# One hybrid encoder layer on one core: an output tile's norm in six parts over the next pair, an opening in another order, a map's weights made earlier

## The chip, the cores and the metric

The kernel runs on one core of a Trainium2 chip. The core's engines take their instructions in order, each from a queue of its own, and meet at semaphores: TensorE (PE; PEld is its weight load), VectorE (DVE), ScalarE (ACT), GpSimd (POOL) and SyncE (SP), whose queue issues most DMAs. The metric is the device time of one execution in microseconds, the median of several runs.

## What is computed

One encoder layer over 4096 tokens of width 1024, with 16 meta tokens put in front and dropped at the end. In the reference, cut:

```python
h = jnp.concatenate([meta, x], axis=1)
u = rmsnorm(h, norm_g[i])
proj = jnp.einsum('bld,de->ble', u, w_in[i])
f_in, f_gate, q, k, v, a_gate = jnp.split(proj, SPLIT_POINTS, axis=-1)
f_out = fourier_branch(f_in, w_fmix[i], b_fmix[i]) * jax.nn.silu(f_gate)
a_out = attention_branch(q, k, v, q_norm_g[i], k_norm_g[i], cos, sin, n_tok) * jax.nn.silu(a_gate)
mixed = jnp.concatenate([f_out, a_out], axis=-1)
h = h + jnp.einsum('ble,ed->bld', mixed, w_out[i])
h = rmsnorm(h, final_g)
return h[:, N_META:]
```

`fourier_branch` is the real part of a 2-D DFT over the positions and the 64 channels of each of 8 groups, followed by a 64 x 64 map of each group. `attention_branch` has 8 query heads and 2 key heads of width 64, with a norm of q and k and a rotary embedding, softmax over all 4112 keys.

## The kernel before

**The first part (up to some 729 us)** projects the tokens in 33 tiles of 128. Operands are split into a high and a low half of 16 bits (`wh`, `wl` for weights, `xh`, `xl` for tokens), and each product takes three matmuls. The first three tiles (meta, 0, 31), the opening, are written out by hand in the order in which their pieces come: `wsplit` makes a quarter of the split weights of a group of columns (`GB` is the last group; ScalarE makes `wh` at line 271, VectorE `wl` at line 272), `tile_q`, `tile_gate` and the like are the matmuls of a tile's columns, `tile_norm` is the norm of q and k on VectorE (lines 355 to 380), `tile_stack` writes keys and values into their layout, `stat` and `stat_end` are the row statistics of the next tiles (squares with a sum on ScalarE at line 201, a root on VectorE from line 211, transposes on TensorE at line 219, a copy at 221), `xload` and `xsplit` load and split a token tile (line 289). After that a loop goes over the remaining tiles with four slots each, in which a table, `plan`, puts the folding of the Fourier weights and the loads for the second part (`at(slot, step)` adds a step).

**The second part (729 us to the end)** has two things in it. First the DFT over positions of one channel group after another (`f_step`), with the group's map (lines 84 to 86: three matmuls with `wvh`, `wvl` and the split transform `thl`); the map's weights are made by `fix_load` (DMAs) and `fix_prep` (VectorE, ScalarE) at the start of this part. Then 32 pairs: a block of 512 queries (b) and two heads (p), each with 66 positions j (33 key tiles, two heads). At a position TensorE makes s (lines 1043 and 1044, two buffers), ScalarE its exp (line 1047), GpSimd or VectorE the remainder `rr` of that exp (line 1049: VectorE at the positions two behind those of the list `AT`, GpSimd at the others), and five positions later TensorE uses them with the values (lines 1064 to 1071). At the sixteen positions of `AT`, TensorE makes two groups of scores for the row maxima of the next pair (line 975, two buffers `m`, both groups behind each other) and VectorE reduces each (line 976).

**The output tile.** Beside this, each pair from the fifth on finishes one output tile of 128 tokens of the block before: transposes at position 12 (`mh` on ScalarE, `ml` on VectorE at 13), the product with the output weights in two halves at positions 15 to 38 and 39 to 62, each ending with `hh` (line 1129). Then the final norm: `square` (ScalarE, line 1141, with the sum of a row in `ss`) at position 62, `root` (ten operations of VectorE on one column, lines 1144 to 1166: a first guess by integer operations and three Newton steps) at position 3 of the next pair, `scale` (VectorE, line 1149, and the store of the tile) at position 14. After the last pair a tail does the last block's tiles.

What sets the order in the second part is the loop itself: instructions reach an engine's queue in the order in which the loop's body writes them, position by position.

Of the kernel before, what the change touches and what calls it, by code (L numbers as in the profile page):

```python
# [22 lines left out]
F32 = mybir.dt.float32  # L23
# [105 lines left out]
def phase_a(tc, a, pool, mm3, id16, id32, sc):  # L129
# [15 lines left out]
    with ExitStack() as st:  # L145
# [359 lines left out]

        PER, SLOTS = 12, 4
# [37 lines left out]
        at(b + 8, ld["acs_load"], 0)  # L544
        done = 27
# [80 lines left out]
        tile_norm(31)  # L626
# [3 lines left out]
        tile_stack(0)  # L630
        wsplit(*GB, 2)
        stat_load(14)
        wsplit(*GB, 3)
        tile_gate(31, 768, fg_d)
        tile_tr(NT)
        stat_store(order[:3])
        tile_stack(31)
# [10 lines left out]
        tile_gate(0, 1280, ag_d)  # L648
        xsplit(15)
        xload(16)  # L650
# [28 lines left out]
def phase_b(tc, a, pool, mm3, id32, id16, sc):  # L679
# [10 lines left out]
    with ExitStack() as st:  # L690
# [53 lines left out]
        wst, wv = (w2.tile([P, 2, 4, P], F32, tag="xr", name=n) for n in ("wst", "wv"))  # L744
        wvh, wvl = (w1.tile([P, 2, 4, P], F16, tag=t, name=n) for t, n in (("mh", "wvh"), ("ml", "wvl")))
# [5 lines left out]
        sgn = bp.tile([P, 2], F32, name="sgn")  # L751
        stk8 = stk8.rearrange("p (g c)->p g c", c=P)

        def fix_load():
            dma(wst, a["wst"])
            dma(sgn, a["sgn"])
            dma(bias, a["bias"])

        def fix_prep():
            V.memset(stk8[0:64], 0.0)  # L760
            V.scalar_tensor_tensor(out=wv[:, 0], in0=wst[:, 0], scalar=sgn[:, 0:1], in1=wst[:, 1],
                                   op0=ALU.mult, op1=ALU.add)
            V.scalar_tensor_tensor(out=wv[:, 1], in0=wst[:, 1], scalar=sgn[:, 0:1], in1=wst[:, 0],
                                   op0=ALU.mult, op1=ALU.add)
            S.activation(wvh, wv, AF.Copy, scale=WS)
            V.scalar_tensor_tensor(out=wvl, in0=wv, scalar=WS, in1=wvh, op0=ALU.mult, op1=ALU.subtract)
# [334 lines left out]
        def out_tr(b, s):  # L1101
# [6 lines left out]
            mh = w1.tile([P, 8, P], F16, tag="mh", name="mh")  # L1108
            ml = w1.tile([P, 8, P], F16, tag="ml", name="ml")
# [24 lines left out]
        def out_end(b, s, d):  # L1134
# [8 lines left out]
            def root():  # L1143
                V.tensor_scalar(out=ss, in0=ss, scalar1=1.0 / D, scalar2=EPS, op0=ALU.mult, op1=ALU.add)
                rsqrt1(sm, rf, ss)
# [7 lines left out]
            return square, root, scale  # L1153

        def rsqrt1(p, y, x):

            t = p.tile([P, 1], F32, tag="r1t", name="r1t")
            h = p.tile([P, 1], F32, tag="r1h", name="r1h")
# [5 lines left out]
            for _ in range(3):  # L1164
                V.tensor_scalar(out=t, in0=y, scalar1=y, scalar2=h, op0=ALU.mult, op1=ALU.mult)
# [65 lines left out]
        for i, (b, p) in enumerate(pairs):  # L1231
# [16 lines left out]
            for j, (qk, pvm) in enumerate(stream(i)):  # L1248
# [26 lines left out]
                if j == TR + 2 and prev:  # L1275
                    prev[2]()
# [199 lines left out]
```

## Time and profile before

| | |
|---|---|
| runs | 3283.27, 3285.66, 3286.85 us; median 3285.66 |
| the profiled execution | 3286.26 us, its span 3284.5 |
| mean granted clock of TensorE | 0.997 |
| TensorE busy (weight loads beside it) | 3216.3 us, 98% (1901.5, 58%) |
| VectorE busy | 2391.6 us, 73% |
| GpSimd busy | 2290.1 us, 70% |
| ScalarE busy | 1701.2 us, 52% |

The rows below are from that one execution. A row of a timeline has the start in us from the span's start, the duration, the engine, the line, the operation, what it writes and reads, and how many such instructions in a row; brackets hold the idle time of the engine just before and what ended it.

### The profile page before, as it was taken

To read this page: it belongs to the slowest core of one execution; us is meant where nothing else is said; L and a number is where in the kernel's file an instruction comes from. 1 tells how busy PE (TensorE), PEld (TensorE's weight loads), DVE (VectorE), ACT (ScalarE), POOL (GpSimd) and SP (SyncE) were. 2 spreads that over 40 slices of the span, in tenths; PEclk is the share of its full clock that TensorE was granted. 3 is DMA by queue.
4 is the path that set the end of the run, shared out by engine and by line. 5 is a ranking of instruction groups with operands and counts; after the bars stand their busy time and mean duration, and the time that the engine had idled before them with its cause. 6 is when DMAs were issued, how large, how long until landed. Compare 5 with 4: busy or idle time off the path is not lost.

```text
span 3284.5 us, 78548 instructions
## 1 busy us (share of the span) xinstructions
PE 3216.3 (98%) x33109; PEld 1901.5 (58%) x33109; DVE 2391.6 (73%) x3225; ACT 1701.2 (52%) x2967; POOL 2290.1 (70%) x2171
## 2 busy tenths in 40 slices
PE   7999999998999999999999999999999999999998
PEld 4555555656666555555555555555555555555564
DVE  6666566437667878777777778877777777887764
ACT  5443443333555555555555555555555555555563
POOL 3655555435777878777777777877787777877762
PEclk9999999999999999999999999999999999999999
DMA  6453343348422220010001000200100010010001
GB/s 223 147 165 128 135 165 109 108 143 260 130 81 84 66 62 27 30 46 21 21 21 47 21 21 24 55 28 21 46 21 21 21 46 21 24 32 25 21 21 58
DMA packets 133848, 225.66 MB, mean 69 GB/s; under 512 B 21654, under 2 KB 76774, under 8 KB 128886
## 3 DMA queue, kind: packets, MB, share of 16 engines
q1 hardware_dynamic: 119670, 195.47, 19.0%
q10 hardware_dynamic: 13824, 25.17, 2.0%
q8 instruction: 259, 4.24, 0.5%
q14 instruction: 95, 0.78, 0.1%
HBM read 159.46 MB, written 61.14 MB: 67 GB/s over the span
## 4 chain that ended last, share of the span: by engine, by line
PE 84%; DVE 10%; ACT 2%; DMA 2%; issue 1%; POOL 1%; SPq 0%; ACTq 0%; DVEq 0%; POOLq 0%
PE s L1043 12%; PE s L1044 12%; PE o L1064 11%; PE po L1124 9%; PE m L975 7%; PE o L1071 7%; PE ps L301 5%; PE ps L302 5%; PE ps L304 4%; DVE mx L976 4%; PE pd L785 3%; PE o L1069 2%; PE o L1067 2%; DVE rr L1049 2%; ACT pe L1047 1%
## 5 line engine op out<-in xcount | busy, mean ns | idle before, releaser
L1049 POOL TENSOR_TENSOR rr<-pe 128x512 f16<-128x512 f32 x1572 | 1712.1, 1105 | 513.2 <-ACT pe L1047 500.7
L1047 ACT ACTIVATE pe<-s 128x512 f32<-128x512 f32 x2112 | 1256.7, 597 | 1042.0 <-PE s L1044 887.9
L976 DVE TENSOR_REDUCE mx<-m 128x2 f32<-128x1024 f32 x1024 | 1205.6, 1219 | 218.6 <-PE m L975 216.8
L1071 PE MATMUL o<-VV,rr 128*128 128x65 f16 x8448 | 975.0, 193 | 2.6 <-POOL rr L1049 2.5
L1071 PEld LDWEIGHTS <-rr 128*128 128x128 f16 x8448 | 784.3, 98 | 174.2 <-POOL rr L1049 5.1
L1064 PE MATMUL o<-VV,pe 128*128 128x129 f16 x6336 | 840.6, 221 | 0.4 <-ACT tt L1075 0.4
L1043 PE MATMUL s<-qA,K 128*128 128x512 f16 x2112 | 799.1, 378 | 14.8 <-ACT pe L1047 14.8
L1044 PE MATMUL s<-qB,K 128*128 128x512 f16 x2112 | 799.7, 379 | 0.9 <-DVE qB L1011 0.9
L1064 PEld LDWEIGHTS <-pe 128*128 128x128 bf16 x6336 | 590.5, 97 | 358.7 <-issue 186.1
L1049 DVE TENSOR_TENSOR rr<-pe 128x512 f16<-128x512 f32 x540 | 479.6, 889 | 228.7 <-ACT pe L1047 226.0
L1067 PE MATMUL o<-VV,pe 128*128 128x65 f16 x2112 | 411.5, 195 | 0.0
L1069 PE MATMUL o<-VV,pe 128*128 128x64 f16 x2112 | 410.3, 194 | 0.0
L301 PE MATMUL ps<-wh,xh 128*128 128x512 f16 (+2 forms) x1032 | 352.8, 354 | 9.2 <-ACT xh L289 9.2
L302 PE MATMUL ps<-wl,xh 128*128 128x512 f16 (+2 forms) x1032 | 352.9, 354 | 7.9 <-DVE wl L272 7.9
L975 PE MATMUL m<-K,qP 64*128 64x512 f16 x2048 | 317.1, 382 | 7.8 <-DVE mx L976 2.8
L304 PE MATMUL ps<-wh,xl 128*128 128x512 f16 x768 | 292.3, 381 | 0.0
L1044 PEld LDWEIGHTS <-K 128*128 128x128 f16 x2112 | 205.1, 97 | 18.5 <-issue 18.3
L1069 PEld LDWEIGHTS <-pe 128*128 128x128 bf16 x2112 | 209.2, 99 | 0.0
L1067 PEld LDWEIGHTS <-pe 128*128 128x128 bf16 x2112 | 206.5, 98 | 0.0
L1043 PEld LDWEIGHTS <-K 128*128 128x128 f16 x2112 | 203.4, 96 | 0.9 <-issue 0.4
L975 PEld LDWEIGHTS <-qP 64*128 64x128 f16 x2048 | 62.2, 94 | 233.9 <-issue 232.1
L290 POOL TENSOR_TENSOR xl<-xt,xh 128x1024 f16<-128x1024 f32 (+1 forms) x33 | 68.7, 2082 | 149.5 <-ACT xh L289 149.3
(207 smaller groups left out, 3683.8 us busy)
## 6 DMA issues: line engine op xcount, KB each, us to landing
ct<-cd SPq DMA_DIRECT2D x16, 1088.0 KB
room<-x SPq DMA_DIRECT2D x32, 512.0 KB
xt<-xt SPq DMA_DIRECT2D x32, 512.0 KB
sg<-fx SPq DMA_DIRECT2D x16, 1024.0 KB
xr<-x SPq DMA_DIRECT2D x32, 512.0 KB
out<-yo SPq DMA_DIRECT2D x32, 512.0 KB
fg_d<-g ACTq DMA_DIRECT2D x32, 256.0 KB
ag_d<-g ACTq DMA_DIRECT2D x32, 256.0 KB
```

The costliest lines, as they stand in the source:

```text
L301: T.matmul(o, xh[:, d, :n], wh[:, d, c0:c1], start=d == 0, stop=False)
L302: T.matmul(o, xh[:, d, :n], wl[:, d, c0:c1], start=False, stop=False)
L975: T.matmul(t[:, e], q[rs, s, p], K[kv][rs, 4 * c:4 * c + 4, 0], start=True, stop=True)
L976: V.tensor_reduce(mx[:, s, :, c], t, axis=AX.X, op=ALU.max)
L1043: T.matmul(s, K[kv][:, t, 0], qa, start=True, stop=False)
L1044: T.matmul(s, K[kv][:, t, 1], qb, start=False, stop=True)
L1047: S.activation(pe, s, AF.Exp, scale=HD ** -0.5)
L1049: eng.tensor_tensor(out=rr, in0=pe, in1=hi, op=ALU.subtract)
L1064: T.matmul(o[:, c0:c0 + 129], hi[:, cs], va, start=t == 0 and s == 0, stop=t == NT, skip_group_check=True)
L1067: T.matmul(o[:, c0:c0 + 65], hi[:, cs], vh, start=False, stop=t == NT, skip_group_check=True)
L1069: T.matmul(o[:, c0:c0 + 64], hi[:, cs], vl, start=False, stop=t == NT, skip_group_check=True)
L1071: T.matmul(o[:, c0:c0 + 65], rr[:, cs], vh, start=False, stop=t == NT, skip_group_check=True)
```

## The change

It has three parts. The norm of an output tile: `root` is cut into `guess` and three `newton` steps, and square, guess, three Newton steps and scale now stand at positions 9, 13, 17, 21, 28 and 32 of the next pair (`NORM`), where square stood at 62 of the pair itself, root at 3 and scale at 14. Behind the last pair the square stands after the first transposes of the tail, the rest after the tail's first two products. The opening: `tile_norm(31)` and `tile_stack(0)` move behind the last two quarters of the weight split, and `tile_gate(0, 1280)`, `xsplit(15)` and `xload(16)` ahead of the statistics. The map's weights: their load and their making move out of the second part into two slots of the token loop, with `wvh` and `wvl` in the buffers of `mh` and `ml`. The diff, cut:

```diff
@@ -503,6 +503,27 @@
+        fix = {}
+
+        def fix_load():
+            fix["wst"] = w1.tile([P, ND, P], F32, tag="pq", name="wst").rearrange("p (e g) c -> p e g c", e=2)
+            fix["sgn"] = wp.tile([P, 2], F32, name="sgn")
+            dma(fix["wst"], a["wst"])
+            dma(fix["sgn"], a["sgn"])
+
+        def fix_prep():
+            wst, sgn = fix["wst"], fix["sgn"]
+            wv = w2.tile([P, ND, P], F32, tag="xt", name="wv").rearrange("p (e g) c -> p e g c", e=2)
+            wvh, wvl = (ld["sh1"].tile([P, 2, 4, P], F16, tag=t, name=n) for t, n in (("mh", "wvh"), ("ml", "wvl")))
+            V.scalar_tensor_tensor(out=wv[:, 0], in0=wst[:, 0], scalar=sgn[:, 0:1], in1=wst[:, 1],
+                                   op0=ALU.mult, op1=ALU.add)
+            V.scalar_tensor_tensor(out=wv[:, 1], in0=wst[:, 1], scalar=sgn[:, 0:1], in1=wst[:, 0],
+                                   op0=ALU.mult, op1=ALU.add)
+            S.activation(wvh, wv, AF.Copy, scale=WS)
+            V.scalar_tensor_tensor(out=wvl, in0=wv, scalar=WS, in1=wvh, op0=ALU.mult, op1=ALU.subtract)
+            ld["wv"] = (wvh, wvl)
+
@@ -542,6 +563,8 @@
         at(b + 8, ld["acs_load"], 0)
+        at(b + 9, fix_load)
+        at(b + 14, fix_prep)
         done = 27
@@ -623,17 +646,20 @@
         wsplit(*GB, 1)
-        tile_norm(31)
         stat_load(15)
...
         tile_gate(0, 768, fg_d)
-        tile_stack(0)
         wsplit(*GB, 2)
...
         wsplit(*GB, 3)
+        tile_norm(31)
+        tile_stack(0)
         tile_gate(31, 768, fg_d)
...
         stat_store(order[:3])
+        tile_gate(0, 1280, ag_d)
+        xsplit(15)
+        xload(16)
         tile_stack(31)
@@ -645,9 +671,6 @@
         weff_load(3)
-        tile_gate(0, 1280, ag_d)
-        xsplit(15)
-        xload(16)
         tile_gate(31, 1280, ag_d)
@@ -741,29 +764,17 @@
-        wst, wv = (w2.tile([P, 2, 4, P], F32, tag="xr", name=n) for n in ("wst", "wv"))
-        wvh, wvl = (w1.tile([P, 2, 4, P], F16, tag=t, name=n) for t, n in (("mh", "wvh"), ("ml", "wvl")))
+        wvh, wvl = ld["wv"]
...
         fgs = {}
-        sgn = bp.tile([P, 2], F32, name="sgn")
         stk8 = stk8.rearrange("p (g c)->p g c", c=P)
         def fix_load():
-            dma(wst, a["wst"])
-            dma(sgn, a["sgn"])
             dma(bias, a["bias"])
-
-        def fix_prep():
             V.memset(stk8[0:64], 0.0)
-            V.scalar_tensor_tensor(out=wv[:, 0], in0=wst[:, 0], scalar=sgn[:, 0:1], in1=wst[:, 1],
-                                   op0=ALU.mult, op1=ALU.add)
-            V.scalar_tensor_tensor(out=wv[:, 1], in0=wst[:, 1], scalar=sgn[:, 0:1], in1=wst[:, 0],
-                                   op0=ALU.mult, op1=ALU.add)
-            S.activation(wvh, wv, AF.Copy, scale=WS)
-            V.scalar_tensor_tensor(out=wvl, in0=wv, scalar=WS, in1=wvh, op0=ALU.mult, op1=ALU.subtract)
@@ -1105,8 +1116,8 @@
                 T.transpose(tv[:, j], src, id32)
-            mh = w1.tile([P, 8, P], F16, tag="mh", name="mh")
-            ml = w1.tile([P, 8, P], F16, tag="ml", name="ml")
+            mh = ld["sh1"].tile([P, 8, P], F16, tag="mh", name="mh")
+            ml = ld["sh1"].tile([P, 8, P], F16, tag="ml", name="ml")
             S.activation(mh, tv, AF.Copy)
@@ -1140,9 +1151,15 @@
-            def root():
+            t = sm.tile([P, 1], F32, tag="r1t", name="r1t")
+            h = sm.tile([P, 1], F32, tag="r1h", name="r1h")
+
+            def guess():
...
-                rsqrt1(sm, rf, ss)
+                root0(rf, ss, t, h)
+
+            def newton():
+                root1(rf, t, h)
@@ -1150,29 +1167,29 @@
-            return square, root, scale
-
-        def rsqrt1(p, y, x):
-
-            t = p.tile([P, 1], F32, tag="r1t", name="r1t")
-            h = p.tile([P, 1], F32, tag="r1h", name="r1h")
+            return square, guess, newton, newton, newton, scale
+
+        def root0(y, x, t, h):
+
...
-            for _ in range(3):
-                V.tensor_scalar(out=t, in0=y, scalar1=y, scalar2=h, op0=ALU.mult, op1=ALU.mult)
-                V.tensor_scalar(out=y, in0=t, scalar1=1.5, scalar2=y, op0=ALU.add, op1=ALU.mult)
+
+        def root1(y, t, h):
+
+            V.tensor_scalar(out=t, in0=y, scalar1=y, scalar2=h, op0=ALU.mult, op1=ALU.mult)
+            V.tensor_scalar(out=y, in0=t, scalar1=1.5, scalar2=y, op0=ALU.add, op1=ALU.mult)
...
         MT, TR, O0, O1 = 60, 12, 15, 39
+        NORM = [9, 13, 17, 21, 28, 32]
         fgb = []
         qload(0, (0,))
-        fix_load()
         f_step(50, 0)
@@ -1185,7 +1202,7 @@
             if n == 1:
-                fix_prep()
+                fix_load()
                 ld["k_load"](ld["rest"])
@@ -1272,13 +1289,10 @@
                     low()
-                if j == TR + 2 and prev:
-                    prev[2]()
+                if j in NORM and prev:
+                    prev[NORM.index(j)]()
                 if j == 62 and b > 0:
                     prev = out_end(b - 1, p, halves[1])
-                    prev[0]()
-                if prev and (j == 3 or j == 65 and i + 1 == len(pairs)):
-                    prev[1]()
                 pend.append(pvm)
@@ -1324,7 +1338,11 @@
-            rsqrt1(sm, rf, ss[:, 0:1])
+            t = sm.tile([P, 1], F32, tag="r1t", name="r1t")
+            h = sm.tile([P, 1], F32, tag="r1h", name="r1h")
+            root0(rf, ss[:, 0:1], t, h)
+            for _ in range(3):
+                root1(rf, t, h)
             S.activation(yo[:, 0:512], xr[:, 0:512], AF.Copy, scale=rf)
@@ -1332,11 +1350,13 @@
         tail_tr(1, 0)
+        prev[0]()
         while pend:
...
         tail_mm(1, 0)
-        prev[2]()
+        for f in prev[1:]:
+            f()
         load_xr(b, 1)
```

TensorE's and GpSimd's queues keep their order. On VectorE, in the opening (`wl` is the low half of the weights, L355 to L380 the norm, `ssq` and `rq` its squares and roots), before:

```order
L272 SCALAR_TENSOR_TENSOR wl<-room,g_107,wh 128x512 x4
L355 TENSOR_REDUCE ssq<-sq 128x10
L356 TENSOR_SCALAR ssq<-ssq 128x10
L170 TENSOR_SCALAR rh_472<-ssq 128x10
L172 TENSOR_SCALAR rq<-rh_472 128x10
...
L359 TENSOR_SCALAR rq<-rq,rw 128x10
L377 TENSOR_TENSOR qs<-t_259,qs 128x8x64
L380 TENSOR_TENSOR ks_113<-t_259,ks_113 128x2x64
L272 SCALAR_TENSOR_TENSOR wl<-room,g_107,wh 128x512 x4
L389 COPY ko<-kt 128x4x16
L221 COPY row<-pr 3x128
```

and now:

```order
L272 SCALAR_TENSOR_TENSOR wl<-room,g_107,wh 128x512 x8
L355 TENSOR_REDUCE ssq<-sq 128x10
L356 TENSOR_SCALAR ssq<-ssq 128x10
L170 TENSOR_SCALAR rh_511<-ssq 128x10
L172 TENSOR_SCALAR rq<-rh_511 128x10
...
L359 TENSOR_SCALAR rq<-rq,rw 128x10
L377 TENSOR_TENSOR qs<-t_259,qs 128x8x64
L380 TENSOR_TENSOR ks_113<-t_259,ks_113 128x2x64
L389 COPY ko<-kt 128x4x16
L221 COPY row<-pr 3x128
```

The second four of the weights' low halves stand ahead of the norm instead of behind it. On ScalarE in the opening, from the last quarters of the weights on (`g` a gate with its store, `qs` and `ks` the scaled q and k, `ss` the sums of the statistics), before:

```order
L271 ACTIVATE wh<-room,g_107 128x512 x4
L367 ACTIVATE g_556<-ps,rw 128x512
L368 DMA fg_d<-g_556 128x512
L376 ACTIVATE qs<-t_304 128x8x64
L378 ACTIVATE ks_112<-t_304 128x2x64
L379 ACTIVATE ks_112<-t_304 128x2x64
L201 ACTIVATE room,ss_134<-room 128x1024 x3
L367 ACTIVATE g_636<-ps,rw 128x512
L368 DMA ag_d<-g_636 128x512
```

and now:

```order
L271 ACTIVATE wh<-room,g_107 128x512 x4
L376 ACTIVATE qs<-t_259 128x8x64
L378 ACTIVATE ks_113<-t_259 128x2x64
L379 ACTIVATE ks_113<-t_259 128x2x64
L367 ACTIVATE g_556<-ps,rw 128x512
...
L367 ACTIVATE g_595<-ps,rw 128x512
L368 DMA ag_d<-g_595 128x512
L289 ACTIVATE xh<-xt 128x1024
L376 ACTIVATE qs<-t_304 128x8x64
L378 ACTIVATE ks_112<-t_304 128x2x64
L379 ACTIVATE ks_112<-t_304 128x2x64
L201 ACTIVATE room,ss_134<-room 128x1024 x3
```

The second gate of tile 0 (`ag_d`) and the split of tile 15 (`xh`) stand ahead of the statistics. On ScalarE, in the pairs, from a finished product of one pair (`tt`) on (`pe` is exp, `xr,ss<-hh` the square), before:

```order
L1047 ACTIVATE pe<-s 128x512 x25
L1075 ACTIVATE tt<-o 128x452
L1047 ACTIVATE pe<-s 128x512 x25
L1141 ACTIVATE xr,ss<-hh 128x1024
L1047 ACTIVATE pe<-s 128x512 x8
L1075 ACTIVATE tt<-o 128x452
L1047 ACTIVATE pe<-s 128x512 x8
L1110 ACTIVATE mh<-m 128x1024
```

and now:

```order
L1058 ACTIVATE pe<-s 128x512 x33
L1086 ACTIVATE tt<-o 128x452
L1058 ACTIVATE pe<-s 128x512 x5
L1152 ACTIVATE xr,ss<-hh 128x1024
L1058 ACTIVATE pe<-s 128x512 x3
L1121 ACTIVATE mh<-m 128x1024
L1058 ACTIVATE pe<-s 128x512 x25
```

The square stood between the last exps of its pair, eight ahead of the next `tt`; it stands now three exps ahead of `mh`, at position 9. On VectorE, from the head of a pair (`mx` reduction of maxima, `rr` remainder, L1144 to L1166 the root, `yo` the scaling), before:

```order
L1049 TENSOR_TENSOR rr<-pe 128x512
L1144 TENSOR_SCALAR ss<-ss 128x1
L1159 TENSOR_SCALAR r1t<-ss 128x1
L1161 TENSOR_SCALAR rf<-r1t 128x1
...
L1166 TENSOR_SCALAR rf<-r1t,rf 128x1
L1077 RECIPROCAL rc<-tt 128x4
L976 TENSOR_REDUCE mx<-m 128x2 x2
L1049 TENSOR_TENSOR rr<-pe 128x512
L976 TENSOR_REDUCE mx<-m 128x2 x2
L1049 TENSOR_TENSOR rr<-pe 128x512
L1112 TENSOR_TENSOR ml<-m,mh 128x1024
L1149 SCALAR_TENSOR_TENSOR yo<-hh,rf,fgb 128x1024
```

and now, the guess with the first Newton step, and further on the scaling:

```order
L1123 TENSOR_TENSOR ml<-m,mh 128x1024
L1158 TENSOR_SCALAR ss<-ss 128x1
...
L1178 TENSOR_SCALAR r1h<-ss 128x1
L987 TENSOR_REDUCE mx<-m 128x2 x2
L1060 TENSOR_TENSOR rr<-pe 128x512
L1182 TENSOR_SCALAR r1t<-rf,r1h 128x1
L1183 TENSOR_SCALAR rf<-r1t,rf 128x1
...
L987 TENSOR_REDUCE mx<-m 128x2 x2
L1060 TENSOR_TENSOR rr<-pe 128x512
L1166 SCALAR_TENSOR_TENSOR yo<-hh,rf,fgb 128x1024
L987 TENSOR_REDUCE mx<-m 128x2 x2
```

The root stood in one piece ahead of the second reduction of the pair and the scaling behind `ml`; each of the parts now stands between a remainder and a reduction, or behind `ml`.

## Rows read from the trace of the kernel before

**Rows 1.** Which engines' work TensorE's instructions waited for over the whole span: line and tile that waited, line and tile waited for, microseconds in total, times, longest.

```profile
PE s L1043 <- ACT pe L1047: 14.8, 31, 1.6
...
PE pr L219 <- DVE rall L177: 2.0, 1, 2.0
```

**Rows 2.** The timeline of TensorE at the end of one pair, and the same stop 26 pairs later: start in us, duration, engine, line, operation, out<-in, and in brackets the idle time before it and what ended it. Rows of other lines lie between.

```profile
1217.97 0.38 PE L1043 MATMUL s<-qA,K 128*128 128x512 f16 x1
...
1219.38 0.38 PE L1043 MATMUL s<-qA,K 128*128 128x512 f16 x1 [0.47 <-ACT pe L1047]
...
1220.17 0.38 PE L1043 MATMUL s<-qA,K 128*128 128x512 f16 x1
...
3158.02 0.38 PE L1043 MATMUL s<-qA,K 128*128 128x512 f16 x1 [0.46 <-ACT pe L1047]
```

**Rows 3.** The timeline of ScalarE at that place.

```profile
1217.70 1.06 ACT L1141 ACTIVATE xr<-hh 128x1024 f32<-128x1024 f32 x1 [0.34 <-DVE hh L1129]
...
1218.75 1.07 ACT L1047 ACTIVATE pe<-s 128x512 f32<-128x512 f32 x2
```

**Rows 4.** The timeline of VectorE at the head of the next pair: the first of the ten small operations of the root, and the reduction that follows them.

```profile
1224.90 0.15 DVE L1144 TENSOR_SCALAR ss<-ss 128x1 f32<-128x1 f32 x1
...
1227.16 2.33 DVE L976 TENSOR_REDUCE mx<-m 128x2 f32<-128x1024 f32 x2
```

**Rows 5.** The timeline of TensorE, the groups for the row maxima at positions 5 and 9 of that pair.

```profile
1225.27 0.61 PE L975 MATMUL m<-K,qP 64*128 64x512 f16 x4
...
1229.05 0.88 PE L975 MATMUL m<-K,qP 64*128 64x512 f16 x4
```

**Rows 6.** The timeline of ScalarE at positions 9 and 10 of that pair.

```profile
1229.22 0.60 ACT L1047 ACTIVATE pe<-s 128x512 f32<-128x512 f32 x1 [0.19 <-PE s L1044]
...
1230.87 0.60 ACT L1047 ACTIVATE pe<-s 128x512 f32<-128x512 f32 x1 [1.05 <-PE s L1044]
```

**Rows 7.** The timeline of GpSimd: one remainder by itself, one while VectorE makes one as well, and the run that follows the four short steps of a finished head.

```profile
1209.14 1.04 POOL L1049 TENSOR_TENSOR rr<-pe 128x512 f16<-128x512 f32 x1 [0.90 <-ACT pe L1047]
...
1224.53 1.35 POOL L1049 TENSOR_TENSOR rr<-pe 128x512 f16<-128x512 f32 x1 [0.53 <-ACT pe L1047]
...
1228.94 13.35 POOL L1049 TENSOR_TENSOR rr<-pe 128x512 f16<-128x512 f32 x11
```

**Rows 8.** The timeline of VectorE: the scaling of the finished tile, at position 14.

```profile
1235.50 1.44 DVE L1149 SCALAR_TENSOR_TENSOR yo<-hh,rf,fgb 128x1024 f32<-128x1024 f32 x1
```

**Rows 9.** The costliest groups of instructions: the remainders that VectorE makes (line, engine, operation, out<-in, count | busy us, mean ns of one | idle time before and what ended it).

```profile
L1049 DVE TENSOR_TENSOR rr<-pe 128x512 f16<-128x512 f32 x540 | 479.6, 889 | 228.7 <-ACT pe L1047 226.0
```

**Rows 10.** The timeline of TensorE in the opening.

```profile
52.25 0.58 PE L302 MATMUL ps<-wl,xh 128*128 128x512 f16 x1 [5.17 <-DVE wl L272]
```

**Rows 11.** The timeline of VectorE in the opening: the first operation of tile 31's norm, and the second half of the last weight columns.

```profile
46.13 0.81 DVE L355 TENSOR_REDUCE ssq<-sq 128x10 f32<-128x640 f32 x1
...
51.45 2.73 DVE L272 SCALAR_TENSOR_TENSOR wl<-room,g,wh 128x512 f16<-128x512 f32 x4
```

**Rows 12.** The busy time by stretch: from and to in us, length, busy us of PE, PEld, DVE, ACT and POOL with their instruction counts, the granted TensorE clock, the DMA share and GB/s.

```profile
52.00:54.00 2.00, 1.75 (x5) 0.64 (x5) 2.00 (x4) 2.00 (x6) 0.00 (x0) 0.50 0.14 23
...
54.00:56.00 2.00, 2.00 (x9) 0.79 (x8) 1.27 (x5) 0.52 (x2) 0.00 (x0) 0.76 0.86 295
...
134.00:136.00 2.00, 2.00 (x6) 0.69 (x5) 1.97 (x3) 1.67 (x2) 0.00 (x0) 0.50 0.05 18
...
744.00:748.00 4.00, 3.43 (x29) 2.76 (x29) 1.65 (x2) 1.19 (x2) 0.80 (x2) 0.57 0.61 197
```

**Rows 13.** The timeline of VectorE: the first operation of the second statistics, and the copy that stands behind them.

```profile
57.62 0.17 DVE L211 TENSOR_SCALAR ss<-ss 128x3 f32<-128x3 f32 x1 [2.35 <-ACT room L201]
...
62.45 0.41 DVE L389 COPY ko<-kt 128x512 f16<-128x512 f16 x1
```

**Rows 14.** The timeline of TensorE: the first transposes of the second and of the third statistics.

```profile
64.42 0.27 PE L219 MATMUL pr<-id,rall 128*3 128x128 f32 x1
...
133.10 0.27 PE L219 MATMUL pr<-id,rall 128*4 128x128 f32 x1 [1.97 <-DVE rall L177]
```

**Rows 15.** The timeline of SyncE's queue: the loads of the first Fourier weights.

```profile
57.88 2.12 SPq L234 DMA_DIRECT2D room<-wft  x3
```

**Rows 16.** The timeline of ScalarE: the split of tile 16.

```profile
74.07 1.06 ACT L289 ACTIVATE xh<-xt 128x1024 f16<-128x1024 f32 x1 [10.63 <-DMA xt<-xt]
```

**Rows 17.** The timeline of TensorE at the first map, and the third wait of the second map.

```profile
741.57 0.22 PE L84 MATMUL s<-wvh,thl 128*128 128x128 f16 x1 [1.52 <-ACT wvh L765]
...
742.83 0.22 PE L85 MATMUL s<-wvl,thl 128*128 128x128 f16 x1 [1.04 <-DVE wvl L766]
...
744.57 0.29 PE L86 MATMUL s<-wvh,thl 128*128 128x128 f16 x1 [1.52 <-DVE thl L826]
...
755.80 0.23 PE L86 MATMUL s<-wvh,thl 128*128 128x128 f16 x1 [0.30 <-DVE thl L826]
```

**Rows 18.** The timeline of ScalarE: the high half of the map's weights.

```profile
740.47 1.06 ACT L765 ACTIVATE wvh<-wv 128x1024 f16<-128x1024 f32 x1 [2.12 <-DVE wv L763]
```

**Rows 19.** The timeline of VectorE in the last token tiles.

```profile
712.79 0.29 DVE L315 TENSOR_TENSOR t<-ps,tab 128x128 f32<-128x128 f32 x1 [5.06 <-ACT vs L335]
```

**Rows 20.** The timeline of TensorE in the last pair and behind it.

```profile
3224.81 0.38 PE L1043 MATMUL s<-qA,K 128*128 128x512 f16 x1 [1.59 <-ACT pe L1047]
...
3229.91 0.39 PE L1309 MATMUL m<-woh,qB 128*128 128x512 f16 x1 [0.89 <-DVE qB L1298]
```

## The prediction

> **What bounds the kernel now.** The profiled run took 3286.26 us, its span 3284.5; the 1.76 around the span stay, and the sum below is made against 3286.26. The median of the three runs, 3285.66, lies 0.6 lower, inside their spread of 3.6. I read the table of busy times first: TensorE is busy for 98% of the span, so only what stops it or lowers its clock can be won. Then the waits of TensorE by what ended them [rows 1]: the largest entry for the pairs is the s matmul waiting for exp on ScalarE, 31 times, 14.8 us. Then the timelines of TensorE, ScalarE, VectorE and GpSimd over one pair, to see where in its 66 positions these waits fall, and last the opening, the first map and the end.
>
> One steady pair lasts (3158.02 - 1219.38) / 26 = 74.56 us [rows 2], 1.13 a position. The s matmul comes every 0.79 us where nothing disturbs (1219.38 to 1220.17), and once in each pair after 1.41 (1217.97 to 1219.38). The difference is 0.62; the listed idle time there is 0.47, so a stop costs some 0.15 more than is listed for it. The cause stands on ScalarE [rows 3]: the square, 1.06 long, at 1217.70, ahead of exp at 1218.75, and TensorE has only two buffers for s.
>
> **The square, from position 62 to position 9 of the next pair.** It leaves the place of the stop. It happens in 27 pairs (26 intervals from the first to the last in rows 2): 27 x 0.62 = 16.7. At position 9 ScalarE is idle for 1.05 between exp at 1229.22 and exp at 1230.87 [rows 6], because the maxima groups hold TensorE for 0.88 then; a square of 1.06 fills just that hole. I cost it at nothing; without that cover it gives the same stop as now.
>
> **The root, from position 3 to 13, 17, 21 and 28.** Ten small VectorE operations begin at 1224.90, and the reduction of position 5's maxima starts behind them at 1227.16 [rows 4], though TensorE had the groups ready at 1225.27 + 0.61 = 1225.88 [rows 5]. The two maxima buffers are then both full when TensorE comes to position 9: its groups take 0.88 there against 0.61 at position 5, 0.27 more. In 26 pairs that is at most 7.0. Whether it all comes back I can't see: GpSimd runs eleven remainders back to back from 1228.94 (13.35 / 11 = 1.21 each, [rows 7]), so it is late itself just there, and TensorE, sooner by 0.27, may wait for it two positions on. Ends 0 and 7.0; I take 0.17 a pair, 4.4, two thirds, as the row of TensorE shows the stop itself while GpSimd's lateness shows in no wait of TensorE's. The root's parts cost four operations at 0.15 (0.6) and, of the 2.26 from 1224.90 to 1227.16, the rest: 1.66, 0.55 for each of the three steps. Position 13's part takes the room of the scaling, which was 1.44 at 1235.50 [rows 8]; the others stand behind a remainder, with a reduction due four positions later.
>
> **The scaling, from 14 to 32.** From position 30's reduction to position 34's there are four positions, 4 x 1.13 = 4.52 us. VectorE has two reductions (2.33, [rows 4]), a remainder (0.89, [rows 9]) and now 1.44 to do: 4.66. It falls 0.14 behind, which the second maxima buffer takes up and the next four positions (3.22 of 4.52) clear. Its store on SyncE's queue moves with it and nothing is queued behind it that a pair needs at once. Cost: nothing.
>
> **The end.** In the last pair the square and root stop TensorE for 1.59 at 3224.81, and the chain behind them makes it wait 0.89 at 3229.91 for qB [rows 20]. With 0.15 for each, 2.8. The root now comes later on VectorE, in front of the last low halves, where 2.26 more could give the second stop back: bound 1.7.
>
> **The map's weights.** At the first map TensorE waits 1.52 for wvh, 1.04 for wvl and 1.52 for thl [rows 17]; wvh itself is made at 740.47, after 2.12 of waiting for wv [rows 18]. From 744 to 748 the granted clock is 0.57 [rows 12], most of it at the 1.2 GHz level: 4 x 0.43 = 1.7 more. Made in the token loop, the weights are there in time; the second map, whose weights are there, still waits 0.30 for its third. So 1.52 + 1.04 + 1.22 + 1.7 = 5.5; some of the clock may fall anyway, since other loads crowd there, and I take 5.0, with 2.5 (the first two waits alone) as the bound. In the loop VectorE has three operations more, each at most the 1.44 of rows 8 long (same 1024 columns), 4.3 together, against an idle time of 5.06 in the last tiles [rows 19]; ScalarE has 1.06. Cost: nothing; uncovered, it delays one tile's chain by 4.3 at the most.
>
> **The opening.** TensorE stops for 5.17 at 52.25, for the low half of the last weight columns [rows 10]. VectorE makes these at 51.45, behind the whole norm of tile 31 that began at 46.13 [rows 11]. Now they come first: the first of four is done at 46.13 + 2.73 / 4 = 46.8, before TensorE asks at 52.25 - 5.17 = 47.08. The stop goes, and with it the granted clock of 0.50 and 0.76 in the two stretches behind it [rows 12]: 2 x 0.50 + 2 x 0.24 = 1.5, of which I count 1.4. TensorE would reach the transposes of the second statistics at 64.42 - 6.57 = 57.85 [rows 14]. But these now wait: their small operations begin on VectorE at 57.62 and are through at 62.45 [rows 13], and tile 0's gate and tile 15's split have moved ahead of the squares. The Fourier weights for the work behind them are issued at 57.88 [rows 15]; the first load can't land at once. The squares of the statistics need 1.06 each and their data; a chain of 4.83 that starts 1.4 earlier ends at 61. I take 62 for TensorE's restart, 2.4 before 64.42, less another 1.4 of lowered clock after a stop of 4 us: gain 1.0. Ends: 64.5 with the lowered clock, -1.6, and 61 with it, +2.0. Tile 16's split on ScalarE waits 10.63 for its data at 74.07 [rows 16]; its load is now issued about 10 us earlier, so the elementwise work has a lead, and the wait of 1.97 at 133.10 for the third statistics (rows 14, and the 2.0 of rows 1) should go, with 0.15 and with the lowered clock behind it (0.50 from 134 to 136, 1.7 with its tail, [rows 12]): 3.8, bound 0. Opening: 1.0 + 3.8 = 4.8, ends -1.6 and 5.8.
>
> **Sum.** 16.7 + 4.4 + 2.8 + 5.0 + 4.8 = 33.7; 3286.26 - 33.7 = 3252.6, so 3253. All good ends: 16.7 + 7.0 + 2.8 + 5.5 + 5.8 = 37.8, 3248.5. All bad ends: 16.7 + 0 + 1.7 + 2.5 - 1.6 = 19.3, 3267.
>
> **Rivals.**
>
> GpSimd takes the place of the maxima buffers. A remainder takes it 1.04 by itself and 1.35 while VectorE makes one [rows 7]; if it is so late in positions 9 to 20 that TensorE meets it, all of the 0.27 comes back as a wait for rr: 4.4 less, 3257. For it: the eleven in a row. Against: TensorE shows no such wait now. Chance 0.25. The Trainium skill, "GPSIMD Engine Reference", section "Key points", says that GpSimd shares its SBUF interfaces with VectorE and contends with VectorE instructions that read two SBUF inputs; that agrees with 1.35 beside 1.04. By that rule the scaling at 32, with hh and fgb as inputs, would slow GpSimd there where it slowed it at 14 before, and the time would be this rival's.
>
> The square stops TensorE at position 9 as it did at 62, because the hole that rows 6 shows is closed once the root no longer delays the groups. Then 16.7 come back, 3269. Against: the groups hold TensorE for 0.61 there in any case, in which no s is made. Chance 0.06.
>
> The opening gives nothing: TensorE waits as long for the statistics as it now does, and the stop at 133.10 stays. 4.8 + 1.6 less, 3259. Chance 0.2.
>
> Slower: the scaling and the three steps, 1.44 + 1.66 = 3.1, stand on the path through VectorE. It decides when VectorE comes to the reduction of position 34 more than one buffer's time late, 2.33: then both maxima buffers are full, TensorE stands, and 27 x 3.1 = 84 are added to a kernel of 3252, 3336. Against: the 4.66 in 4.52 above, and idle time before the reductions. Chance 0.02.
>
> **How the numbers follow.** My forecast, with all its terms near the values taken, 0.47; GpSimd 0.25; the opening 0.2; the square 0.06; slower 0.02. The first three lie in 3245 to 3262, the square's at the edge; 3245 (the good ends, less the run spread of 3.6) to 3268 (the bad ends) hold over 8 in 10, and no narrower range takes in the bounds. 0.2%, 6.6 us, is about what a measurement can tell from no change: faster means below 3279.1, slower above 3292.2. Even the bad ends are faster. Faster 0.95, the same 0.03 (stops that come back in several places at once), slower 0.02.
>
> **What would show it.** Right: the s matmul's waits for exp shrink from 14.8 to under 3; the interval at positions 64 to 65 is 0.79; the groups at position 9 take 0.61; a pair lasts 73.7 to 73.8; no wait for wl at 52, for wvh and wvl at 741, for rall at 133. Wrong: waits for rr that were not there (GpSimd), an s wait at positions 9 to 11 with the square ahead of exp (the square), waits of the maxima groups at 34 to 42 (VectorE), or a stop before the statistics' transposes near 60 that ends at 64 or later.

## The result and the profile after

The changed kernel takes 3252.29 us (median of four runs, 3250.57 to 3252.61) against 3285.52 for the kernel before, a ratio of 0.9898 with a 95% interval of 0.9881 to 0.9916: faster by 1.0%. Its profiled execution took 3252.05 us with a span of 3250.3, that of before 3284.5, so 34.2 us lie between the two traces. Of the times further down, one median (the kernel without the map part) has a single execution of 13040 us among its five, which its interval leaves out.

The waits of TensorE in the changed kernel: engine, tile and line that waited, what it waited for, us in total, times, longest. Ahead of them stands only the wait for the split of a token tile (`xh`, 8.7, before 9.2).

```profile
PE pd L796 <- DMA ct<-cd: 3.9, 2, 3.6
PE pr L219 <- DVE rall L177: 2.8, 1, 2.8
PE ps L302 <- DVE wl L272: 2.7, 5, 1.4
...
PE s L1054 <- ACT pe L1058: 1.0, 4, 0.3
```

The wait for exp, 14.8 us in 31 stops in [rows 1], is down to 1.0 in 4. The wait for `wl` no longer holds the 5.17 of [rows 10]. The wait for `ct`, a load of the DFT's tables, has doubled (1.9 before), and the one for `rall` is another than in [rows 1]: it stands at the second statistics, where the 2.0 stood at the third.

The timeline of TensorE at the end of the pair of [rows 2] (the s matmuls of positions 64 and 65), the maxima groups at positions 5 and 9 of the next pair, and the s matmul of position 65, 26 pairs later.

```profile
1209.94 0.38 PE L1054 MATMUL s<-qA,K 128*128 128x512 f16 x1
1210.72 0.38 PE L1054 MATMUL s<-qA,K 128*128 128x512 f16 x1
...
1216.60 0.60 PE L986 MATMUL m<-K,qP 64*128 64x512 f16 x4
...
1220.38 0.61 PE L986 MATMUL m<-K,qP 64*128 64x512 f16 x4
...
3126.16 0.38 PE L1054 MATMUL s<-qA,K 128*128 128x512 f16 x1
```

The interval at position 65 is 1210.72 - 1209.94 = 0.78, where it was 1.41. The groups at position 9 take 0.61, where they took 0.88 [rows 5]. A pair lasts (3126.16 - 1210.72) / 26 = 73.67, 0.89 less: the whole of 0.62 and the whole of 0.27.

The timelines of ScalarE and of VectorE in the same pair: the square with the exps around it; then the reduction of position 5, the first operation of the guess, the three Newton steps (first operation of each), the scaling and the reduction of position 34.

```profile
1220.55 0.60 ACT L1058 ACTIVATE pe<-s 128x512 f32<-128x512 f32 x1 [0.19 <-PE s L1055]
1221.04 1.05 ACT L1152 ACTIVATE xr<-hh 128x1024 f32<-128x1024 f32 x1
...
1222.08 1.28 ACT L1058 ACTIVATE pe<-s 128x512 f32<-128x512 f32 x2
```

```profile
1217.14 2.33 DVE L987 TENSOR_REDUCE mx<-m 128x2 f32<-128x1024 f32 x2
...
1226.56 0.14 DVE L1158 TENSOR_SCALAR ss<-ss 128x1 f32<-128x1 f32 x1
...
1231.44 0.26 DVE L1182 TENSOR_SCALAR r1t<-rf,r1h 128x1 f32<-128x1 f32 x1
...
1235.31 0.27 DVE L1182 TENSOR_SCALAR r1t<-rf,r1h 128x1 f32<-128x1 f32 x1
...
1243.59 0.27 DVE L1182 TENSOR_SCALAR r1t<-rf,r1h 128x1 f32<-128x1 f32 x1
...
1248.24 1.28 DVE L1166 SCALAR_TENSOR_TENSOR yo<-hh,rf,fgb 128x1024 f32<-128x1024 f32 x1
1249.49 2.36 DVE L987 TENSOR_REDUCE mx<-m 128x2 f32<-128x1024 f32 x2
```

The square starts 0.49 after the start of the exp ahead of it and fills the hole that [rows 6] showed. The reduction of position 5 starts at 1217.14, with its groups (1216.60 + 0.60 = 1217.20); before, it came 1.28 late.

The opening and the first two maps: TensorE's stops, from its timeline, and the first matmul of the first map, which has none.

```profile
61.07 0.27 PE L219 MATMUL pr<-id,rall 128*3 128x128 f32 x1 [2.77 <-DVE rall L177]
...
733.29 0.22 PE L84 MATMUL s<-wvh,thl 128*128 128x128 f16 x1
...
743.74 0.23 PE L86 MATMUL s<-wvh,thl 128*128 128x128 f16 x1 [0.30 <-DVE thl L837]
...
745.27 0.23 PE L86 MATMUL s<-wvh,thl 128*128 128x128 f16 x1 [0.69 <-POOL thl L838]
```

```profile
762.20 2.03 PE L796 MATMUL pd<-acs,ct 128*128 128x264 f16 x12 [3.56 <-DMA ct<-cd]
```

And the busy time by stretch (columns as in [rows 12]: the last three are the granted clock, the DMA share and GB/s).

```profile
60.00:62.00 2.00, 0.88 (x6) 0.73 (x7) 1.28 (x7) 1.57 (x3) 0.00 (x0) 1.00 0.87 274
62.00:64.00 2.00, 2.00 (x13) 1.12 (x12) 1.27 (x4) 0.92 (x5) 1.89 (x1) 1.00 0.83 257
...
764.00:768.00 4.00, 4.00 (x26) 2.50 (x25) 2.34 (x3) 1.23 (x2) 0.38 (x1) 0.69 0.99 396
...
1122.00:1124.00 2.00, 2.00 (x18) 1.34 (x17) 2.00 (x3) 0.10 (x1) 0.00 (x0) 0.50 0.02 8
```

The three waits of the first map, 4.08 in [rows 17], are gone. The two stops at 743.74 and 745.27 belong to the second map: the 0.30 is the one that [rows 17] shows at 755.80, and the 0.69, for the part of `thl` that GpSimd makes, is new. The wait for `ct`, 1.88 at the same matmul in the trace of before, is 3.56. Stages of the two traces, in us gained: up to the first DFT matmul 6.9 (it starts at 728.81 before and at 721.92 now), from there to the first s matmul 3.2 (76.4 to 73.2), up to pair 4 a loss of 1.9 (most of it 1.5 at 1122, where the granted clock is at 0.50, behind waits that the trace of before has as well, at a clock of 1.00), from there to pair 31 23.7, and 2.4 behind it.

### The profile page after: what moved, and what is told of

It is laid out like the page before. It is cut to its first block, busy times and chain, and to the rows that moved or that the text cites. A ratio compares the mean times of both kernels' runs of the same rounds, so it can differ in the third digit from the quotient of the medians.

```text
span 3250.3 us, 78527 instructions
## 1 busy us (share of the span) xinstructions
PE 3204.9 (99%) x33109; PEld 1896.5 (58%) x33109; DVE 2370.2 (73%) x3225; ACT 1702.8 (52%) x2967; POOL 2266.7 (70%) x2171
## 4 chain that ended last, share of the span: by engine, by line
PE 94%; DVE 2%; DMA 1%; ACT 1%; POOL 1%; issue 1%; SPq 0%; ACTq 0%; POOLq 0%; DVEq 0%
PE s L1055 14%; PE s L1054 14%; PE o L1075 12%; PE po L1135 9%; PE m L986 8%; PE o L1082 8%; PE ps L301 6%; PE ps L302 6%; PE ps L304 5%; PE pd L796 2%; PE o L1080 2%; PE o L1078 2%; PE m L1323 1%; PE pf L84 1%; PE pf L85 1%; PE pf L86 1%
## 5 line engine op out<-in xcount | busy, mean ns | idle before, releaser
L1060 POOL TENSOR_TENSOR rr<-pe 128x512 f16<-128x512 f32 x1572 | 1687.9, 1091 | 514.0 <-ACT pe L1058 507.8
L1060 DVE TENSOR_TENSOR rr<-pe 128x512 f16<-128x512 f32 x540 | 457.4, 848 | 231.1 <-ACT pe L1058 226.8
L1135 PE MATMUL po<-woh,mh 128*128 128x512 f16 x448 | 169.8, 379 | 0.9 <-DVE hh L1140 0.9
```

Source lines behind the costliest of these rows:

```text
L1060: eng.tensor_tensor(out=rr, in0=pe, in1=hi, op=ALU.subtract)
```

## The experiments

The unit of a stage is taken from the traces (start of the same matmul in both); the median tells the whole.

**The three parts, each alone** on the kernel before. The edits are the three parts of the diff.

> Only the norm in six parts, opening and map as before. By the waits of TensorE: the s matmul's stop at the end of a pair (0.62 in 27 pairs) and the longer maxima groups at position 9 (0.27 in 26 pairs) go, a pair lasts 73.7, and 2.4 go at the end: 23.7 + 2.4 = 26.1 less, 3259.4. If GpSimd took the place of the maxima buffers the pairs would give only 16.7: 3266.4, with waits for rr.

Measured: 3257.56 against 3284.47, 0.9919 (0.9905 to 0.9932): 26.9 less. A pair lasts 73.67 (here and below over the same 26 pairs as above), there is no new wait for `rr`, the gain in the pairs is whole.

> Only the opening's new order. The stops of 5.17 at 52 and of 1.97 at 133 go with the lowered clock behind them, and one of about 2.8 before the transposes of the second statistics comes: 6.9 less, 3278.6, if the opening's gain doesn't depend on the other parts. The rival, that the lowered clock is only a matter of chance in each run: a gain of 4 to 5, 3281, with 0.50 granted somewhere between 58 and 66.

Measured: 3278.11, 0.9979 (0.9970 to 0.9988): 6.4 less, near the 6.9 expected. But the trace (of the slowest of the eleven executions, 3282.57) had the rival's mark too:

```profile
60.54 0.27 PE L219 MATMUL pr<-id,rall 128*3 128x128 f32 x1 [2.75 <-DVE rall L177]
```

```profile
62.00:64.00 2.00, 2.00 (x6) 0.73 (x5) 1.27 (x4) 0.92 (x4) 2.00 (x2) 0.50 0.88 301
64.00:66.00 2.00, 2.00 (x8) 0.79 (x7) 0.00 (x0) 0.21 (x1) 2.00 (x5) 0.78 0.96 248
```

The same stop as in the changed kernel (2.75 and 2.77), and this time the clock went to its 1.2 GHz level behind it. So whether it falls is not settled by the program: the rival was right in that.

> Only the map's weights made in the token loop. The three waits at the first map shrink from 4.08 to about 1 and the lowered clock from 744 to 748 goes, 5.5 less; the wait for ct near 770 grows from 1.88 by about 1.7 and gives some back: 3.3 less, 3282.2. If the wait for ct grew in the changed kernel only because its opening is shorter, it stays at 1.88 here and the gain is 5.0: 3280.5.

Measured: 3285.05 against 3284.47, 1.0000 (0.9991 to 1.0009): nothing, where 3.3 were expected. The parts alone give 26.9 + 6.4 - 0.6 = 32.7 of the 33.2 that they give together. The trace of the map part has none of the three waits at the first map, but the growing wait for `ct`, and at 133 the stop of the statistics as before, this time without a lowered clock:

```profile
133.99 0.27 PE L219 MATMUL pr<-id,rall 128*4 128x128 f32 x1 [2.00 <-DVE rall L177]
...
769.02 1.28 PE L796 MATMUL pd<-acs,ct 128*128 128x264 f16 x5 [3.86 <-DMA ct<-cd]
```

**The square back at 62.**

```diff
-        NORM = [9, 13, 17, 21, 28, 32]
+        NORM = [13, 17, 21, 28, 32]
...
                 if j == 62 and b > 0:
                     prev = out_end(b - 1, p, halves[1])
+                    prev[0]()
...
```

> The changed kernel with the square back at position 62 of its own pair, all else as changed. By the stop that the square makes ahead of exp: the interval at position 65 is 1.41 again, 27 x 0.62 = 16.7 more, 3269.0, and the groups at position 9 stay at 0.61 (the root's part stays won). If the gain of the pairs came from the root alone, 3252 stays. If square and root only won together: 23.7 more, 3276.

Measured: 3275.16, 22.9 above the changed kernel; the third branch, not my theory's 16.7. A pair lasts 74.50, all but the 74.56 of before. The timeline of GpSimd in pair 10 of this kernel, its last short step for a finished head and the remainders behind it; and that of TensorE where it uses them:

```profile
1588.79 1.02 POOL L1093 TENSOR_TENSOR ob<-ob,rc 128x256 f32<-128x256 f32 x1
1589.76 4.48 POOL L1060 TENSOR_TENSOR rr<-pe 128x512 f16<-128x512 f32 x4
```

```profile
1591.61 0.22 PE L1075 MATMUL o<-VV,pe 128*128 128x129 f16 x1
1591.85 0.20 PE L1082 MATMUL o<-VV,rr 128*128 128x65 f16 x1
```

The groups at position 9 stay short (the 0.27 is won there), but at position 11 TensorE waits for the remainder: from 1591.61 to 1591.85, where these two stand 0.06 apart elsewhere; the position lasts 0.99 and not 0.79, which takes 0.20 of the 0.27 back. The remainders start 9.18 us after the pair's first s matmul (at 1580.58); in the changed kernel they start after 8.49, with the last short step at 0.62 instead of 1.02. So the first rival of the prediction is real while the square stands at 62, and with the square gone GpSimd is early enough for all of it.

**The root in one piece, and all of it early.** `NORM` becomes [9, 13, 13, 13, 13, 32] and [9, 13, 13, 13, 13, 14], with the steps of one position called behind each other.

> The changed kernel with the guess and the three Newton steps in one piece at position 13, the scaling at 32. If the cutting into parts matters, 1.66 more stand ahead of the reduction of position 15 (after ml) and the maxima groups of position 23 or the remainders wait: some 0.1 to 0.3 in 26 pairs, 3255 to 3260. If only the place matters (away from position 3, where a reduction is due at once), nothing changes: 3252, since the scaling of 1.44 stood there before without a stop.

Measured: 3250.85, 0.9901 (0.9888 to 0.9915), a pair of 73.67. The cutting of the root costs nothing and brings nothing; its place is what counts.

> The changed kernel with root and scaling in one piece at positions 13 and 14: ml, root and scaling, 1.23 + 2.26 + 1.44 = 4.9 on VectorE between two reductions. By the two maxima buffers, VectorE may be 2.33 late: it has some 4.5 - 2.33 - 0.9 = 1.3 of room in four positions and is late by more than 2.33, so TensorE stops at position 19 or 23 for 0.5 to 1.5 in 26 pairs: 3265 to 3291. If VectorE's room is larger than that, 3252.

Measured: 3279.05, 26.8 above the changed kernel; a pair lasts 74.68. The timelines of VectorE and of TensorE in pair 10:

```profile
1601.97 1.28 DVE L1166 SCALAR_TENSOR_TENSOR yo<-hh,rf,fgb 128x1024 f32<-128x1024 f32 x1
1603.18 2.35 DVE L987 TENSOR_REDUCE mx<-m 128x2 f32<-128x1024 f32 x2
```

```profile
1604.62 0.39 PE L986 MATMUL m<-K,qP 64*128 64x512 f16 x2
1605.58 0.39 PE L986 MATMUL m<-K,qP 64*128 64x512 f16 x2 [0.57 <-DVE mx L987]
```

The reduction of position 15 starts at 1603.18, behind `ml`, root and scaling; both maxima buffers are full when TensorE comes to position 19, and it stops. With the root at 13 the scaling has to leave 14: that is what its move to 32 is for.

**The scaling three times** (each writes the same values).

```diff
-                V.scalar_tensor_tensor(out=yo, in0=hh, scalar=rf, in1=fgb[0], op0=ALU.mult, op1=ALU.mult)
+                for _ in range(3):
+                    V.scalar_tensor_tensor(out=yo, in0=hh, scalar=rf, in1=fgb[0], op0=ALU.mult, op1=ALU.mult)
```

> The changed kernel with the scaling at position 32 written three times (the same values again), 4.32 in place of 1.44. This tests the rival on the slower side: VectorE would come to the reduction of position 34 some 3.0 late, over the 2.33 that the second maxima buffer covers, and TensorE stops for about 0.7 in 27 pairs, 3271; with the next stretches too full to catch up, up to 2.9 x 27 = 78, 3330. If VectorE has more room than the sum of durations says: 3252.

Measured: 3314.71, 62.4 above the changed kernel and slower than before (1.0097, 1.0082 to 1.0113). In pair 10:

```profile
1624.89 5.24 DVE L1167 SCALAR_TENSOR_TENSOR yo<-hh,rf,fgb 128x1024 f32<-128x1024 f32 x3
1630.05 2.34 DVE L987 TENSOR_REDUCE mx<-m 128x2 f32<-128x1024 f32 x2
```

```profile
1631.32 0.39 PE L986 MATMUL m<-K,qP 64*128 64x512 f16 x2 [0.88 <-DVE mx L987]
1632.45 0.39 PE L986 MATMUL m<-K,qP 64*128 64x512 f16 x2 [0.74 <-DVE mx L987]
```

The slower rival's mechanism, at its place, position 38: 3.96 more on VectorE (5.24 - 1.28) lengthen this pair by 2.07, and 22 of the 26 by as much. In the other four the granted clock falls behind the same stops (0.90 and 0.74 in pair 12, where 0.88 and 0.74 stand above), and the pair is 1.4 to 1.7 longer still. In pair 12:

```profile
1786.00:1788.00 2.00, 2.00 (x14) 1.10 (x12) 1.93 (x2) 0.61 (x2) 2.00 (x3) 0.50 0.67 155
```

VectorE can be about 1.9 later there (3.96 - 2.07) before TensorE feels it, less than the 2.33 the prediction took as the point from which it decides. The single scaling stays under it.

**Two tries at what is left.** First the squares and the root of the second statistics ahead of tile 15's split and tile 31's stack:

```diff
         tile_gate(0, 1280, ag_d)
+        for c, t in enumerate((15, 16, 14)):
+            stat(t, ss0, 3 + c)
         xsplit(15)
         xload(16)
+        stat_end(order[3:6], ss0[:, 3:6])
         tile_stack(31)
...
-            stat(t, ss0, 3 + c)
             weff_load(c)
-        stat_end(order[3:6], ss0[:, 3:6])
```

> The changed kernel with the squares and the root of the second statistics ahead of the split of tile 15 and of tile 31's stack in the program. If the stop of 2.77 at 61 comes from the squares standing behind that work on ScalarE and VectorE, it shrinks to 0 to 1.5, and the time by 1.3 to 2.8: 3249.5 to 3251. If the data of the third tile lands late, the stop stays near 2.8 and the time at 3252, or grows where tile 15's split is late instead.

Measured: 3255.22, 0.9911 (0.9894 to 0.9927), 2.9 more than the changed kernel; in the trace the first s matmul comes 4.7 later. The stop before `pr` grew to 3.90, and it no longer ends with the statistics:

```profile
62.71 0.27 PE L219 MATMUL pr<-id,rall 128*3 128x128 f32 x1 [3.90 <-DVE ko L389]
```

The timelines of VectorE and of GpSimd show where the earlier start went:

```profile
55.60 2.13 DVE L177 SCALAR_TENSOR_TENSOR rall<-rt,rall 128x3 f32<-128x3 f32 x1
...
59.24 0.16 DVE L177 SCALAR_TENSOR_TENSOR rall<-rt,rall 128x3 f32<-128x3 f32 x1
...
60.12 2.21 DVE L380 TENSOR_TENSOR ks<-t,ks 128x128 f16<-128x128 f32 x1
62.25 0.41 DVE L389 COPY ko<-kt 128x512 f16<-128x512 f16 x1
```

```profile
55.59 2.13 POOL L290 TENSOR_TENSOR xl<-xt,xh 128x1024 f16<-128x1024 f32 x1 [1.60 <-ACT xh L289]
...
59.96 2.21 POOL L290 TENSOR_TENSOR xl<-xt,xh 128x1024 f16<-128x1024 f32 x1 [1.56 <-ACT xh L289]
```

The statistics started at once. One of the root's steps on three columns, 0.16 long in most places, took 2.13, as long as GpSimd's subtraction beside it; still the root was done at 59.40 (59.24 + 0.16), where the changed kernel has it at 60.93. But tile 31's stack now stands behind it on VectorE, its `ks` is held for 2.21 as well, and `ko`, the copy behind that, is done at 62.66, which is what TensorE then waited for. The stop moved to the work that the statistics were put ahead of.

Second the load of qA and qB behind one more load of `ct` (in the traces 32.0 us after the first DFT matmul, in the changed kernel 25.0), and both edits together:

```diff
-            elif n == 4:
+            elif n == 8:
                 qload(0, (1,))
```

> The changed kernel with the load of the first block's qA and qB (1.5 MB) issued some 15 us later, behind two more loads of ct. If the wait of 3.56 for ct at 762 comes from the queue of bytes ahead of it, 1.5 MB at about 400 GB/s is 3.8 us: the wait goes, with the clock of 0.69 behind it (1.2): 3.5 to 4.8 less, 3247.5 to 3249. If ct waits for something else (its buffer, its own 1.1 MB), nothing changes: 3252.

Measured: 3247.48, 0.9887 (0.9873 to 0.9902), the fastest of all. The wait for `ct` at 762 is gone; at a later load one of 1.30 has come:

```profile
768.55 1.52 PE L796 MATMUL pd<-acs,ct 128*128 128x264 f16 x12 [1.30 <-DMA ct<-cd]
```

From the first DFT matmul to the first s matmul it takes 70.1 where the changed kernel took 73.2. The rest of the difference between the medians (4.8) lies within the intervals.

> Both of the last two edits on the changed kernel: the gains add if they are stops of TensorE in places far apart, 5 to 7.6 less, 3245 to 3247. If a gain in the opening only makes the wait for ct longer, as the map's did, no better than the later load alone: 3248.

Measured: 3251.03, 0.9900 (0.9885 to 0.9915): the first edit costs here about what it cost alone (3.6 and 2.9; the stop before `pr` is 3.90 again and ends with `ko`), and the second gives what it gave (70.6 in the same stage).

**The map part once more**, left out of the changed kernel, with the load of qA and qB at its old place and later.

> The changed kernel without its map part (norm and opening as changed, the map's weights made at the start of the second part as before). The map's weights alone moved the median by nothing that can be told. If its gain at the first map is given back in the wait for ct, this kernel takes the changed kernel's 3252 within 3. If the map part is worth 3 to 5, 3255 to 3257.

Measured: 3252.33, 0.9908 (0.9893 to 0.9923): the changed kernel's time. From the first DFT matmul to the first s matmul 73.3, against 73.2 with the map part.

> The same without the map part, with the later load of qA and qB. With the bytes ahead of ct gone, the changed kernel took 3247.5. If the map part's gain was only hidden by the wait for ct, it shows here: 5.5 more, 3253. If the map part is worth nothing even then, 3247.5.

Measured: 3252.34, 0.9908 (0.9894 to 0.9921), and 73.5 in that stage. In its trace the first map has its old waits, with a lowered clock behind them, and no wait for `ct` at all:

```profile
734.66 0.22 PE L84 MATMUL s<-wvh,thl 128*128 128x128 f16 x1 [1.72 <-ACT wvh L765]
```

```profile
736.00:740.00 4.00, 2.53 (x24) 2.35 (x24) 2.73 (x3) 0.60 (x1) 0.61 (x1) 0.50 0.83 287
```

With the qA and qB load at its old place the map part is worth 0.1 in the stage, and with that load out of the way 3.4 (73.5 to 70.1). Each is one trace against one, and without the map part the same stage took 72.8 (norm alone), 76.4 (before) and 78.5 (opening alone) in other traces; what decides are the medians, 3252.29 against 3252.33 with the load at its old place, 3247.48 against 3252.34 with the load later. TensorE, some 5 us sooner at the next `ct`, only waits for it longer, until the bytes queued ahead of it are out of the way.

## Why the prediction was right, term by term

The time (3253 forecast, 3252.29 measured) and the sign were right; of the terms two were too small and one too large, and they made up for each other. So far it is luck that the sum came within 1 us.

- **The pairs**, 16.7 + 4.4 = 21.1 forecast, 23.7 in the trace. Both stops went, at the places named. The mis-sized term is the 0.17 of 0.27 for the root: all of 0.27 came back. I took GpSimd's back-to-back run as something that stays; part of it came from the square itself, as the square's return to 62 shows (0.20 of the 0.27 lost to the wait for `rr`). The two terms were priced one by one, but the root's move is worth 0.27 only with the square moved, and 0.07 without. What the square's move is worth with the root left at 3 was not run.
- **Cover of the moved steps**, forecast at nothing: right. The square lies in the hole at position 9, the root's parts and the scaling stop nothing. The prediction saw that position 13's part takes the room of the scaling, but put no price on leaving the scaling at 14 beside a whole root, which the 26.8 us show; it weighed only whether 32 has room.
- **The end**, 2.8 forecast, 2.4 in the trace.
- **The opening**, 4.8 forecast, 6.9 in the trace and 6.4 by the median of that part alone, above the upper end of 5.8. The stop at 52 and the one at 133 went; TensorE restarted at 61.07, not 62; and the 1.4 of lowered clock behind that new stop was not paid in this trace. The restart was near for a wrong reason. The prediction let a chain of 4.83 start 1.4 earlier; it started at 58.58, 0.96 later than before, behind the work now ahead of its squares, but its root was done in 2.35, at 60.93, because the 4.83 had in it a step that GpSimd held up (its rows stand in the last section) and the changed kernel has none there. The lowered clock was paid in others: behind a stop of 2.5 to 3.0 at this place the granted clock fell in five of nine profiles with this opening, and not in four. The expected price is about half of what I took.
- **The map's weights**, 5.0 forecast, nothing measured alone. The waits went as forecast, and the third one whole, where the prediction let 0.30 of it stay. The step that failed is the one that left the wait for `ct` where it was when TensorE arrives sooner. The loads set the pace there (a DMA share of 0.99 from 764 to 768); the trace of before showed 1.88 of that wait, and the profile of the norm part alone, with the same map, showed none. The bound of 2.5 for this term should have been 0.
- **The rivals.** GpSimd: it takes the stop's place only with the square at 62. The scaling at 32 does slow GpSimd, as the prediction says by its rule (the remainder at 1248.62, beside the scaling of 1248.24, takes 1.80 where 1.04 is usual), but TensorE does not wait for it. The square at position 9: refuted. The opening's gain not realised: refuted. The slower one: it exists, and needs about 1.9 more on VectorE; it was right to give it little.

## What to carry to other kernels

A stop that is removed from a stage in which loads set the pace is given back at the next load: look for what the transfer ahead of it is, and move that first. Two stops a few positions apart in one loop are priced together, since the one may be what makes the other engine late. Where a step is moved into a busy engine's stretch, ask what must leave that stretch in turn; cutting a chain of small operations into parts was worth nothing here, and its place everything.

## What the runs showed of the hardware that was not expected

The same stop of TensorE is followed by the 1.2 GHz level in one run and not in another: 2.75 us (granted 0.50 behind it) and 2.77 (1.00); at 133 a stop of 1.97 in the kernel before (0.50, [rows 12]) and of 2.00 in the kernel with the map part alone, which keeps 1.00 from 134 to 136:

```profile
134.00:136.00 2.00, 2.00 (x10) 0.97 (x11) 1.97 (x3) 0.85 (x2) 0.00 (x0) 1.00 0.41 147
```

The stops of position 38 with the scaling three times show the same within one run: four pairs of 26 at 0.50 behind them, the others at 1.00. A price for the lowered clock, some 1.4 to 1.7 us here, is a chance and not a term.

A VectorE operation of 0.16 us with two inputs in SBUF took 2.13 while GpSimd ran an operation of 2.13, and ended 0.01 behind it; one that takes 0.28 in most places took 2.21 beside one of 2.21, and ended 0.16 behind it. The kernel before has the same in the chain of 4.83 that the prediction used, in the timelines of VectorE and of GpSimd:

```profile
59.81 2.04 DVE L177 SCALAR_TENSOR_TENSOR rall<-rt,rall 128x3 f32<-128x3 f32 x1
```

```profile
59.70 2.13 POOL L290 TENSOR_TENSOR xl<-xt,xh 128x1024 f16<-128x1024 f32 x1 [8.31 <-ACT xh L289]
```

The Trainium skill, "GPSIMD Engine Reference", section "Key points", names this contention of GpSimd and VectorE instructions with two SBUF inputs; these rows agree, and they show that the short one can be held for the whole of the long one.
